# A two-layer hybrid decoder on one core: splitting its float32 weights in the DMA queue of GpSimd instead of on VectorE

## The chip, the core and the metric

The kernel runs on one core of one Trainium2 chip. The metric is the device time of one execution in microseconds (us); less is better. A core has TensorE (PE; the loading of its weights is listed as PEld), VectorE (DVE), ScalarE (ACT), GpSimd (POOL) and SyncE (SP); 16 DMA engines move data between HBM and the core's SBUF.

## The reference

Two post-norm layers over 528 tokens (16 learned ones and 512 real ones) of 2048 channels. A layer is one input projection, three groups of heads that read it side by side, and one output projection:

```python
proj = h @ w_in                                   # 2048 x 5120
c, q, k, v, gates, r_x = split(proj)
y_conv = pointwise(silu(norm(dwconv(glu(c))))) * silu(gate)
y_attn = sliding_window_attention(rope(q), rope(k), v, sinks) * silu(gate)
y_lru  = rg_lru(conv4(r_x)) * silu(gate)
mixed  = concat(y_conv, y_attn, y_lru) @ w_out    # 2048 x 2048
h      = layer_norm(ALPHA * h + mixed)
```

All of it is float32. The last layer gives back the 512 real tokens only.

## The kernel before

**The products.** TensorE takes its operands as float32r, a float32 that is rounded to fewer bits. So every operand is held as two tiles, `hi` (the value rounded) and `lo` (what the rounding left), and a product is three matmuls: hi times hi, hi times lo, lo times hi (`mm3`, L403). The stream (the tokens' channels) is kept with 128 channels on the partitions, so a layer's input is 16 pairs of tiles of 128 x 528.

**The weights.** `weight_list` (L1178) lays all weights in the order of use: 40 column tiles of `w_in`, 4 of the pointwise weight and the output projection, for each layer. A weight is 128 x 2048 float32 in HBM. `weight_load` (L374) loads it in pieces of 128 x 1024 (512 KB) on SyncE's queue into one of two raw buffers (pool `w`). `weight_split` (L382) cuts a piece into halves of 512 columns. For each half it takes two tiles of the pool `u`: ScalarE copies the raw half into the first with rounding, and VectorE subtracts that from the raw half into the second:

```python
yield S(out=wh, in_=r, func=AF.Copy)
yield V("tensor_tensor", out=wl, in0=r, in1=wh.bitcast(F32), op=ALU.subtract)
```

There are 456 halves in all. One half serves 4 of the 16 steps of a product's sum, that is 24 matmuls where the 528 tokens are two ranges of 264 (layer 0, and the first 16 weights of layer 1: 292 halves) and 12 matmuls of 512 columns otherwise. `flow["held"]` counts pairs that are allotted and not yet used up; no more than `flow["ahead"]` are held: 5 as a rule, 14 in the first group of layer 0 (three products side by side, `gemms`, L424), 18 at the end of layer 0 and in the first group of layer 1, 16 in the last chunk of the output.

**The order of the work.** The program is a set of threads (generators). The class `Sched` (L95) merges them into one fixed order for each engine: it takes the step that could start first by an estimate of costs and latencies. Each engine then runs its list in that order and waits by semaphores. An instruction that waits holds back all that stand behind it on its engine; that goes for the DMA issues in SyncE's and GpSimd's lists as well.

**The start.** `x_load` (L475) brings the tokens on SyncE's queue, `x_norm` normalises them, `turn` (L530) transposes them on TensorE and splits them: ScalarE to a tile `t`, VectorE rounds it to `hi`, and the subtraction to `lo` (L547) is GpSimd's for three channel tiles of four. There are four buffers `t`. The first group of products runs in two phases: tokens 0 to 255 (matmuls of 256 columns), then the other 272.

**The end of layer 0.** `output` (L932): 13 products one after another, then the last three side by side in two phases of 264 tokens, with residual and norm behind them on VectorE.

**GpSimd** does nothing else but the subtractions of the start and 8 operations at the very end.

Of the kernel before, what the change touches and what calls it, by code (L numbers as in the profile page):

```python
# [25 lines left out]
NUNITS = 78  # L26
NRAW = 2
# [3 lines left out]
# column tiles of w_in, in the order in which the permutation below lays them out  # L31
# [11 lines left out]
# per-channel parameters: column offsets in the packed array  # L43
# [7 lines left out]
# constants: rope cos, rope sin, band mask of the first block, band mask, identity  # L51
# [3 lines left out]
# query blocks: (first token, queries, pieces of keys, value chunks, mask)  # L55
# [9 lines left out]
# the branches' tiles that are attention's, among recurrence, attention, convolution, attention  # L65
# [29 lines left out]
class Sched:  # L95
    """Threads of instructions (generators), merged into one order per engine by an estimate of when each could start."""
# [16 lines left out]
    # -- tiles --  # L113
# [19 lines left out]
    # -- instructions --  # L133
# [62 lines left out]
    # -- threads --  # L196
# [76 lines left out]
def body(tc, nc, ctx, t):  # L273
# [5 lines left out]
    cp, up, wp, sp_, ap_ = pool("const", 1), pool("units", 1), pool("wraw", 1), pool("small", 1), pool("attn", 1)  # L279
    pp = pool("psum", 1, space=PSUM)  # L280
    k = Sched(tc, nc, {"u": (up, None, NUNITS), "w": (wp, (128, 1024), NRAW), "s": (sp_, (128, 24), 8), "a": (ap_, (128, 4, L), 2), "P": (ap_, (128, L), 8), "t": (ap_, None, 4), "p": (pp, (128, 2, 512), 2), "b": (pp, (128, 512), 4)})
    V, S, G = k.V, k.S, k.G

# [23 lines left out]
    def prepare():  # L307
        """Small parameters worked out once."""
# [4 lines left out]
        for l in range(DEPTH):  # L313
# [3 lines left out]
            # 2 * softplus(-lam) = 2 * (max(-lam, 0) + log1p(exp(-|lam|)))  # L317
# [21 lines left out]
    class Product:  # L339
        """A product in PSUM: pieces of tokens, in banks of one tile or of several."""  # L340
# [10 lines left out]
        def views(self, x):  # L351
            """Pairs of (product, its place in a tile of tokens)."""
            if self.rngs == FULL and len(self.tiles) == 1:
                return [(self.tiles[0][:, :, 0:HALF], x[:, 0:L].rearrange("p (h c) -> p h c", h=2))]
            return [(self.bank(i), x[:, c:c + n]) for i, (_, c, n) in enumerate(self.rngs)]
# [17 lines left out]

    def weight_load():  # L374
        for w, i in pieces:
            m = min(1024, w.src.shape[1] - 1024 * i)
            raw = yield Alloc("w")
            yield k.dma(raw[:, 0:m], w.src[:, 1024 * i:1024 * i + m])
            w.raw.append((raw, m))
            flow["loaded"] += 1  # L380

    def weight_split():  # L382
        for w, i in pieces:
            yield Until(lambda: len(w.raw) > i)
            raw, m = w.raw[i]
            for j in range(0, m, 512):
                yield Until(lambda: flow["held"] < flow["ahead"])
                flow["held"] += 1
                k.wheld = flow["held"]
                wh = yield Alloc("u", F32R, 512, True)  # L390
                wl = yield Alloc("u", F32R, 512, True)
                r = raw[:, j:j + 512]
                yield S(out=wh, in_=r, func=AF.Copy)
                yield V("tensor_tensor", out=wl, in0=r, in1=wh.bitcast(F32), op=ALU.subtract)
                w.parts.append((wh, wl))
            k.release(raw)
# [11 lines left out]
    def gemm(xs, rngs):  # L408
        """sum over k of w[k].T @ xs[k], w the next weight of the stream, xs pairs of parts."""
# [14 lines left out]
    def gemms(count, xs, phases, ready, done, first):  # L424
        """Several products side by side, the tokens in phases; first: all products for each k in turn, read when all is done."""
# [168 lines left out]
    def means(x):  # L594
        """Means over the channels of four tiles from their sum, exact parts against an exact weight."""
# [62 lines left out]
    def keys(y, p, pr):  # L658
        """Both parts of a pair of key heads, twice over the partitions; for the later blocks the meta keys are put before each window."""
# [74 lines left out]
    def scores(y):  # L734
        """Query by key products and their softmax, block by block."""
# [40 lines left out]
    def mix(y):  # L776
        """Probabilities times values; the four query heads of a key head side by side."""
# [43 lines left out]
    def recur(y, j, pr):  # L821
        """Short convolution, gates and the linear recurrence of one tile of channels."""
# [29 lines left out]
        # a = exp(-2 h), sqrt(1 - a * a) = sqrt(tanh(h)) * (1 + a) with h = c * softplus(-lam) * sigmoid / 2  # L852
# [14 lines left out]
    def gate(y, j, pr):  # L867
        """branch * silu(gate), split for the output product."""
# [19 lines left out]
    def project(y, x, ready, phases):  # L888
        """The products of a layer's input projection, in order."""
# [42 lines left out]
    def output(y, x, nx):  # L932
        """Output product with channels on partitions; residual and the norm over channels follow behind."""
# [29 lines left out]
        def gather():  # L963
            """Sums over channels of z less a first mean, and of its square."""
# [199 lines left out]
    with tc.manual_schedule():  # L1164
# [6 lines left out]
        k.run()  # L1171


# passes of the last output product: (chunk of columns, token tiles)
LAST = [(0, [0, 1, 2, 3]), (1, [0, 1, 2, 3]), (2, [0, 1, 2, 3]), (3, [0, 1]), (3, [2]), (3, [3])]


# [110 lines left out]
```

## Time and profile before

| | |
|---|---|
| time of the runs, median (lowest to highest) | 1491.61 us (1491.59 to 1491.63) |
| profiled execution, span | 1493.8 us |
| TensorE busy | 1454.3 us, 97% |
| VectorE busy | 1052.9 us, 70% |
| ScalarE busy | 706.3 us, 47% |
| GpSimd busy | 33.4 us, 2% |
| HBM read | 128.12 MB |

The profile is of one execution. Its span, first to last instruction, is all the profile gives of that execution's time; it is 2.2 us (0.15%) above the median of the runs. Busy time of TensorE is not TensorE at its peak, since matmuls overlap; the number of matmuls in a stretch (the count behind each busy time) tells its pace. In the rows below, `u` are the tiles of the pool `u`, `w` the raw weight buffers, `a` and `P` hold tokens at the start, `t` the tiles of the turn, `p` and `b` are PSUM.

### The profile page before, as it was taken

To read this page: it belongs to the slowest core of one execution; us is meant where nothing else is said; L and a number is where in the kernel's file an instruction comes from. 1 tells how busy PE (TensorE), PEld (TensorE's weight loads), DVE (VectorE), ACT (ScalarE), POOL (GpSimd) and SP (SyncE) were. 2 spreads that over 40 slices of the span, in tenths; PEclk is the share of its full clock that TensorE was granted. 3 is DMA by queue.
4 is the path that set the end of the run, shared out by engine and by line. 5 is a ranking of instruction groups with operands and counts; after the bars stand their busy time and mean duration, and the time that the engine had idled before them with its cause. 6 is when DMAs were issued, how large, how long until landed. Compare 5 with 4: busy or idle time off the path is not lost.

```text
span 1493.8 us, 25183 instructions
## 1 busy us (share of the span) xinstructions
PE 1454.3 (97%) x10028; PEld 1353.5 (91%) x10028; DVE 1052.9 (70%) x2103; ACT 706.3 (47%) x1539; POOL 33.4 (2%) x36
## 2 busy tenths in 40 slices
PE   4999999999999999999999999999999999999996
PEld 3999999999999999999999997998788888888885
DVE  7788999985588444364688889999747864433438
ACT  5422448884377332222368134778735853323211
POOL 2200000000000000000000000000000000000003
PEclk9999999999999999999999999999999999999998
DMA  6312422142222223232433034223332223523323
GB/s 230 94 51 91 135 79 78 58 135 93 85 73 70 85 86 106 75 103 86 127 115 92 24 108 124 78 60 116 92 101 85 71 71 97 157 85 113 108 62 112
DMA packets 56549, 142.32 MB, mean 95 GB/s; under 512 B 12465, under 2 KB 20913, under 8 KB 56433
## 3 DMA queue, kind: packets, MB, share of 16 engines
q1 hardware_dynamic: 56432, 140.73, 30.8%
q8 instruction: 78, 1.28, 0.4%
q14 instruction: 39, 0.31, 0.1%
HBM read 128.12 MB, written 4.19 MB: 89 GB/s over the span
## 4 chain that ended last, share of the span: by engine, by line
PE 86%; DVE 8%; DMA 2%; ACT 2%; issue 1%; SPq 0%; ACTq 0%; DVEq 0%
PE p L184 68%; PE b L184 16%; DVE u L160 5%; DVE a L160 2%; PE b L188 2%; ACT u L174 1%; DMA w<-in_win 1%; DVE s L160 1%; SPq L194 0%; DMA u<-u 0%; DMA a<-in_x 0%; DVE t L160 0%; ACT t L174 0%; DVE P L160 0%; PE p L188 0%
## 5 line engine op out<-in xcount | busy, mean ns | idle before, releaser
L184 PE MATMUL p<-u,u 128*128 128x264 f32 (+3 forms) x7824 | 1183.1, 306 | 5.7 <-DVE u L160 2.9
L184 PEld LDWEIGHTS p<-u,u 128*128 128x128 f32 x7824 | 1066.5, 189 | 63.2 <-DVE u L160 4.6
L160 DVE TENSOR_TENSOR u<-w,u 128x512 fp32r<-128x512 f32 x456 | 306.3, 690 | 171.3 <-ACT u L174 163.3
L174 ACT ACTIVATE u<-w 128x512 fp32r<-128x512 f32 x456 | 273.1, 622 | 237.6 <-DMA w<-in_wout 118.9
L184 PE MATMUL b<-u,u 128*128 128x512 f32 (+6 forms) x1568 | 291.0, 325 | 4.3 <-DVE u L160 2.7
L184 PEld LDWEIGHTS b<-u,u 128*128 128x128 f32 (+2 forms) x1568 | 241.8, 185 | 33.9 <-DVE u L160 4.3
L160 DVE SCALAR_TENSOR_TENSOR a<-u,dp,a 128x527 f32<-128x527 f32 (+14 forms) x240 | 179.8, 750 | 4.2
L174 ACT ACTIVATE P<-P,s 100x257 f32<-100x257 f32 (+5 forms) x240 | 111.2, 479 | 28.7 <-DVE s L160 28.6
L160 DVE TENSOR_TENSOR u<-u,u 128x528 f32<-128x528 f32 (+5 forms) x146 | 100.9, 697 | 20.8 <-ACT u L174 17.9
L174 ACT ACTIVATE u<-p 128x528 f32<-128x528 f32 (+2 forms) x71 | 42.4, 598 | 152.1 <-PE p L184 151.8
L174 ACT ACTIVATE u<-u 64x528 fp32r<-64x528 f32 (+5 forms) x112 | 63.8, 584 | 81.1 <-DVE u L160 75.1
L160 DVE SCALAR_TENSOR_TENSOR u<-u,p 128x528 f32<-128x528 f32 (+3 forms) x45 | 30.8, 684 | 74.3 <-ACT u L174 53.4
L174 ACT ACTIVATE t<-b 128x400 fp32r<-128x400 f32 (+3 forms) x112 | 57.1, 510 | 44.2 <-PE b L184 22.0
L160 DVE CUSTOM_DVE_ANT_0 P<-b,con,nsink 100x256 f32<-100x256 f32 (+2 forms) x160 | 67.3, 451 | 3.0 <-PE b L184 2.2
L160 DVE TENSOR_TENSOR t<-b,t 128x400 fp32r<-128x400 f32 (+2 forms) x72 | 41.7, 580 | 13.5 <-ACT t L174 13.2
L184 PE MATMUL b<-t,u 128*128 128x400 f32 (+2 forms) x144 | 50.5, 351 | 0.0
L167 POOL TENSOR_TENSOR u<-u,P 128x512 f32<-128x512 f32 x8 | 13.1, 1649 | 1412.5 <-ACT u L174 1412.4
L188 PE MATMUL b<-con,P 100*128 100x100 f32 (+2 forms) x320 | 44.1, 253 | 0.0
L174 ACT ACTIVATE u<-b 128x256 fp32r<-128x256 f32 (+4 forms) x28 | 11.8, 443 | 58.5 <-PE b L188 52.0
L188 PEld LDWEIGHTS b<-con,P 100*128 100x128 f32 (+2 forms) x320 | 36.0, 140 | 3.1 <-DVE s L160 0.4
L160 DVE TENSOR_SCALAR P<-P,s 100x256 f32<-100x256 f32 (+3 forms) x88 | 31.6, 364 | 0.7
L160 DVE SCALAR_TENSOR_TENSOR u<-u,u 128x528 f32<-128x528 f32 (+1 forms) x40 | 27.5, 699 | 5.1 <-ACT u L174 4.7
(103 smaller groups left out, 692.1 us busy)
## 6 DMA issues: line engine op xcount, KB each, us to landing
w<-in_win SPq DMA_DIRECT2D x160, 512.0 KB, 3.7
w<-in_wout SPq DMA_DIRECT2D x64, 512.0 KB, 3.8
u<-u SPq DMA_DIRECT2D x48, 120.0 KB, 2.1
a<-in_x SPq DMA_DIRECT2D x8, 256.0 KB, 6.0
P<-in_x SPq DMA_DIRECT2D x8, 256.0 KB, 6.0
u<-u SPq DMA_DIRECT2D x16, 128.0 KB, 2.1
w<-in_pw SPq DMA_DIRECT2D x8, 256.0 KB, 2.6
out<-a SPq DMA_DIRECT2D x8, 256.0 KB, 2.3
```

Of the source, the lines that this page charges most:

```text
L160: return self._op("V", c, outs, ins, lambda: f(**kw))
L167: return self._op("G", c, outs, ins, lambda: f(**kw))
L174: op = self._op("S", c, outs, ins, lambda: f(**kw))
L184: return self._op("T", c, [out], [w, x], lambda: f(out, w, x, start=start, stop=stop))
L188: return self._op("T", max(2 * self._size(ident) / 2400, 0.11) + 0.005, [out], [x, ident], lambda: f(out, x, ident))
```

## The change

The raw buffers and their pool go (the pool `u` gets 81 tiles in place of 78). A half is now loaded by a DMA that GpSimd issues, from HBM straight into the float32r tile `wh`, rounding on the way. ScalarE writes minus that into `wl`. A second DMA of GpSimd reads the same half from HBM once more and adds it onto `wl`. VectorE takes no part. The scheduler's entry for such a DMA is a cost of 1.0 us on GpSimd and 3.0 us of latency. Comments and docstrings are deleted too, which changes nothing.

```diff
-NUNITS = 78
-NRAW = 2
+NUNITS = 81
...
+    def gdma(self, out, in_, add=False):
+
+        f = self.nc.gpsimd.dma_start
+        kw = dict(accum_op=ALU.add) if add else {}
+        ins = [out] if add else []
+        return self._op("G", 1.0, [out], ins, lambda: f(out=out, in_=in_, **kw), 3.0)
...
-    cp, up, wp, sp_, ap_ = pool("const", 1), pool("units", 1), pool("wraw", 1), pool("small", 1), pool("attn", 1)
+    cp, up, sp_, ap_ = pool("const", 1), pool("units", 1), pool("small", 1), pool("attn", 1)
...
+    halves = [(w, j) for w, i in pieces for j in range(1024 * i, min(1024 * i + 1024, w.src.shape[1]), 512)]
+    loading = []
+
     def weight_load():
-        for w, i in pieces:
-            m = min(1024, w.src.shape[1] - 1024 * i)
-            raw = yield Alloc("w")
-            yield k.dma(raw[:, 0:m], w.src[:, 1024 * i:1024 * i + m])
-            w.raw.append((raw, m))
-            flow["loaded"] += 1
+
+        for w, j in halves:
+            yield Until(lambda: flow["held"] < flow["ahead"])
+            flow["held"] += 1
+            k.wheld = flow["held"]
+            wh = yield Alloc("u", F32R, 512, True)
+            wl = yield Alloc("u", F32R, 512, True)
+            yield k.gdma(wh, w.src[:, j:j + 512])
+            loading.append((wh, wl))
+            flow["loaded"] += 0.5
 
     def weight_split():
-        for w, i in pieces:
-            yield Until(lambda: len(w.raw) > i)
-            raw, m = w.raw[i]
-            for j in range(0, m, 512):
-                yield Until(lambda: flow["held"] < flow["ahead"])
-                flow["held"] += 1
-                k.wheld = flow["held"]
-                wh = yield Alloc("u", F32R, 512, True)
-                wl = yield Alloc("u", F32R, 512, True)
-                r = raw[:, j:j + 512]
-                yield S(out=wh, in_=r, func=AF.Copy)
-                yield V("tensor_tensor", out=wl, in0=r, in1=wh.bitcast(F32), op=ALU.subtract)
-                w.parts.append((wh, wl))
-            k.release(raw)
+
+        for n, (w, j) in enumerate(halves):
+            yield Until(lambda: len(loading) > n)
+            wh, wl = loading[n]
+            yield S(out=wl, in_=wh.bitcast(F32), func=AF.Copy, scale=-1.0)
+            yield k.gdma(wl, w.src[:, j:j + 512], add=True)
+            w.parts.append((wh, wl))
```

In the lists below a DMA row names the tile that it writes (pool, buffer and a serial number); of a pair of one half, the load carries the smaller serial number and the adding DMA the next one. `waits` names the semaphores of the engine or DMA lane that the row waits for.

**The start, GpSimd.** Before, its list begins with the subtractions of `turn`, which write the `lo` tiles (`u1`, `u3`, `u5`):

```order
L1284 UNCONDITIONAL_BRANCH [waits barrier_Pool_Activation_PE_DVE_SP_gather]
L167 ISA
L167 TENSOR_TENSOR u1_2_88<-t0_64_204,u0_1_87 128x256 [waits DVE_49]
L167 TENSOR_TENSOR u3_4_90<-t1_65_207,u2_3_89 128x256 [waits DVE_49]
L167 TENSOR_TENSOR u5_6_92<-t2_73_223,u4_5_91 128x256 [waits DVE_49]
```

Now 14 loads and 14 adding DMAs of the first group stand ahead of them; the last of these and the first subtractions are:

```order
L200 DMA u53_68_190<-in_win 128x512 [waits DMASW0_49,Activation_49]
L200 DMA u55_76_205<-in_win 128x512 [waits DMASW1_49,Activation_49]
L200 DMA u57_78_212<-in_win 128x512 [waits DMASW2_49,Activation_49]
L200 DMA u59_80_219<-in_win 128x512 [waits DMASW3_49,Activation_49]
L166 ISA
L166 TENSOR_TENSOR u1_2_85<-t0_89_242,u0_1_84 128x256 [waits DVE_49]
L166 TENSOR_TENSOR u3_4_87<-t1_90_246,u2_3_86 128x256 [waits DVE_49]
L166 TENSOR_TENSOR u5_6_89<-t2_94_262,u4_5_88 128x256 [waits DVE_49]
```

So the `lo` tiles of the tokens moved behind the last adding DMA, which waits for ScalarE. On ScalarE the last passes stand behind the square root of the norm of the last 16 tokens (`s2`):

```order
L173 ACTIVATE s2_93_255<-s2_93_255,cst_74 16x1 [waits DVE_49]
L173 ACTIVATE u55_76_205<-u54_75_204 128x512 [waits DMASW3_49]
L173 ACTIVATE u57_78_212<-u56_77_211 128x512 [waits DMASW4_49]
L173 ACTIVATE u59_80_219<-u58_79_218 128x512 [waits DMASW5_49]
L173 ACTIVATE t0_101_337<-b3_98_299,par_70 128x256 [waits PE_49,Pool_49]
```

What moved: the chain from the last tokens' norm to the first `lo` tile now runs through GpSimd's list.

**In the course of a layer, GpSimd.** Before, its list has nothing here; SyncE's list holds the loads of whole pieces, each waiting for VectorE to be done with the raw buffer:

```order
L194 DMA w0_202_1222<-in_win 128x1024 [waits DMAHW3_49,DVE_49]
L194 DMA w1_207_1285<-in_win 128x1024 [waits DMAHW5_49,DVE_49]
L194 DMA w0_214_1352<-in_win 128x1024 [waits DMAHW6_49,DVE_49]
```

Now loads (they wait for TensorE to free a pair) and adding DMAs (they wait for ScalarE) alternate in one list:

```order
L200 DMA u56_206_1471<-in_win 128x512 [waits DMASW1_49,PE_49]
L200 DMA u58_208_1503<-in_win 128x512 [waits DMASW2_49,PE_49]
L200 DMA u55_203_1438<-in_win 128x512 [waits DMASW3_49,Activation_49]
L200 DMA u57_207_1472<-in_win 128x512 [waits DMASW4_49,Activation_49]
L200 DMA u64_210_1536<-in_win 128x512 [waits DMASW5_49,PE_49]
L200 DMA u59_209_1504<-in_win 128x512 [waits DMASW6_49,Activation_49]
L200 DMA u66_212_1568<-in_win 128x512 [waits DMASW7_49,PE_49]
```

What moved: an adding DMA (`u55`, `u57`) now stands behind one or two later loads, which wait for TensorE.

**The end of layer 0.** Before, VectorE's list holds the subtractions of the weights between those of the residual; the first row here is the residual's of channel tile 12:

```order
L160 TENSOR_TENSOR u20_1219_8840<-u24_25_111,u25_26_112 128x528
L160 TENSOR_TENSOR u33_1218_8839<-w0_1211_8763,u40_1217_8838 128x512 [waits DMAHW1_49,Activation_49]
L160 TENSOR_TENSOR u49_1222_8846<-w0_1211_8763,u21_1221_8845 128x512 [waits Activation_49]
L160 TENSOR_TENSOR u5_1225_8851<-w1_1216_8812,u4_1224_8850 128x512 [waits DMAHW2_49,Activation_49]
L160 TENSOR_TENSOR u15_1227_8856<-w1_1216_8812,u14_1226_8855 128x512 [waits Activation_49]
```

Now 15 loads stand in a row on GpSimd, for the last three products and for the first group of layer 1, and the adding DMAs of all of them behind; the last three loads and the first three adding DMAs are:

```order
L200 DMA u24_1127_8889<-in_win 128x512 [waits DMASW1_49,DVE_49,Pool_49]
L200 DMA u9_1129_8892<-in_win 128x512 [waits DMASW2_49,PE_49]
L200 DMA u57_1131_8895<-in_win 128x512 [waits DMASW3_49,PE_49]
L200 DMA u6_1100_8768<-in_wout0 128x512 [waits DMASW4_49,Activation_49]
L200 DMA u34_1102_8797<-in_wout0 128x512 [waits DMASW5_49,Activation_49]
L200 DMA u13_1104_8825<-in_wout0 128x512 [waits DMASW6_49,Activation_49]
```

What moved: `u6`, needed by the first of the three products, now comes behind the load into `u57`, a buffer that TensorE frees in the product before.

## Rows read from the trace of the kernel before

**Rows 1.** Stretches: each engine's busy us (instructions), granted clock, DMA share, GB/s.

```profile
core 0: us, PE busy (x) PEld busy (x) DVE busy (x) ACT busy (x) POOL busy (x), PEclk, DMA share, GB/s
0.00:25.00 25.00, 7.84 (x28) 4.90 (x28) 17.63 (x42) 13.43 (x24) 4.89 (x10) 1.00 0.80 269
...
225.00:275.00 50.00, 50.00 (x411) 49.56 (x410) 48.97 (x134) 43.32 (x125) 0.00 (x0) 1.00 0.22 67
...
600.00:700.00 100.00, 100.00 (x819) 99.87 (x818) 49.64 (x77) 23.49 (x41) 0.00 (x0) 1.00 0.27 85
...
1225.00:1275.00 50.00, 50.00 (x218) 40.62 (x217) 19.43 (x30) 14.94 (x26) 0.00 (x0) 1.00 0.29 94
```

**Rows 2.** What TensorE waited for, whole span: us in total, times, longest.

```profile
PE b L188 <- ACT a L174: 13.1, 2, 11.3
PE p L184 <- DVE u L160: 3.6, 5, 1.3
PE b L188 <- ACT t L174: 3.0, 4, 2.2
PE b L184 <- DVE u L160: 2.7, 3, 1.6
PE p L184 <- ACT u L174: 2.6, 2, 1.9
```

**Rows 3.** Instructions on the raw buffers: count, ns min/median/max, first and last start.

```profile
L174 ACT ACTIVATE u<-w x456: 612/620/650, 13.6 to 1433.4; 128x512 fp32r<-128x512 f32 x152
L160 DVE TENSOR_TENSOR u<-w,u x456: 628/687/1230, 14.3 to 1434.7; 128x512 fp32r<-128x512 f32 x152
...
DMA to landing us min/median/max: 2.5/3.7/7.1
```

**Rows 4.** The start, in order of time: start us, us, engine, line, instruction.

```profile
0.74 3.71 SPq L194 DMA_DIRECT2D a<-in_x  x8
...
18.72 0.74 POOL L167 TENSOR_TENSOR u<-t,u 128x256 fp32r<-128x256 f32 x1 [18.27 <-DVE u L160]
...
20.29 1.86 POOL L167 TENSOR_TENSOR u<-t,u 128x256 fp32r<-128x256 f32 x2 [0.83 <-DVE u L160]
...
20.34 1.23 DVE L160 TENSOR_TENSOR u<-w,u 128x512 fp32r<-128x512 f32 x1
```

**Rows 5.** Matmuls of L184 alone in two stretches: PE busy (x), PEld busy (x), clock, DMA.

```profile
18.00:34.10 16.10, 8.40 (x27) 6.62 (x28) 1.00 0.44 120
34.10:75.60 41.50, 36.26 (x263) 32.85 (x261) 1.00 0.37 121
```

**Rows 6.** The chain that ended last, around the end of the first group.

```profile
69.68 5.83 DMA w<-in_win
...
75.53 0.63 ACT u L174
...
77.39 22.74 PE p L184 x172
```

**Rows 7.** DMA issues of the whole span: KB each, median us from issue to landing.

```profile
w<-in_wout SPq DMA_DIRECT2D x64, 512.0 KB, 3.8
...
P<-in_x SPq DMA_DIRECT2D x8, 256.0 KB, 6.0
...
w<-in_pw SPq DMA_DIRECT2D x8, 256.0 KB, 2.6
```

**Rows 8.** The DMA queue from 340 to 346 us, one 256 KB load: packets, MB, share.

```profile
q1 hardware_dynamic: 144, 0.26, 16.6%
```

**Rows 9.** The stretch 3 to 17 us, as in Rows 1.

```profile
3.00:17.00 14.00, 1.70 (x6) 0.86 (x6) 9.44 (x20) 6.60 (x12) 0.00 (x0) 1.00 0.97 351
```

**Rows 10.** GpSimd's groups by form: count | busy us, mean ns of one | idle before.

```profile
L167 POOL TENSOR_TENSOR u<-u,P 128x512 f32<-128x512 f32 x8 | 13.1, 1649 | 1412.5 <-ACT u L174 1412.4
...
L167 POOL TENSOR_TENSOR u<-t,u 128x256 fp32r<-128x256 f32 x12 | 10.4, 885 | 23.8 <-DVE u L160 23.8
```

**Rows 11.** VectorE's scaling by a constant for each partition, from the page.

```profile
L160 DVE TENSOR_SCALAR P<-P,s 100x256 f32<-100x256 f32 (+3 forms) x88 | 31.6, 364 | 0.7
```

More of the change, by code (lines that the diff above doesn't have):

```diff
@@ L277, in pool @@
         return ctx.enter_context(tc.tile_pool(name=name, bufs=bufs, **kw))
-    cp, up, wp, sp_, ap_ = pool("const", 1), pool("units", 1), pool("wraw", 1), pool("small", 1), pool("attn", 1)
+    cp, up, sp_, ap_ = pool("const", 1), pool("units", 1), pool("small", 1), pool("attn", 1)
     pp = pool("psum", 1, space=PSUM)
-    k = Sched(tc, nc, {"u": (up, None, NUNITS), "w": (wp, (128, 1024), NRAW), "s": (sp_, (128, 24), 8), "a": (ap_, (128, 4, L), 2), "P": (ap_, (128, L), 8), "t": (ap_, None, 4), "p": (pp, (128, 2, 512), 2), "b": (pp, (128, 512), 4)})
+    k = Sched(tc, nc, {"u": (up, None, NUNITS), "s": (sp_, (128, 24), 8), "a": (ap_, (128, 4, L), 2), "P": (ap_, (128, L), 8), "t": (ap_, None, 4), "p": (pp, (128, 2, 512), 2), "b": (pp, (128, 512), 4)})
     V, S, G = k.V, k.S, k.G
```

## The prediction

> **What bounds the kernel now.** First the table of stretches. TensorE is busy without a gap in all that lies behind the start, at full clock, and its count of matmuls gives the pace: 819 of 264 columns in 100 us, so 0.122 us each, and 218 of 512 columns in 50 us, so 0.229 us [rows 1]. A half of a weight feeds 24 of the first or 12 of the second kind. It is used up in 24 x 0.122 = 2.93 us, or in 12 x 0.229 = 2.75 us; that is the rate at which the new path must deliver. VectorE at 49 of 50 us does not slow TensorE: from 225 to 275 us there are 411 matmuls in 50 us, the full pace [rows 1]. Second, the waits: TensorE waits for VectorE only 3.6 + 2.7 = 6.3 us in the whole run; the longest item, 13.1 us, is the first transposes, which wait for the tokens [rows 2]. So the 306 us of VectorE that go (456 subtractions of 0.687 us [rows 3]) are worth 6.3 us at most: they are hidden already. More than the wait of the start can't be won at all. A measurement of this kernel tells about 2% from no change, 30 us; a gain of that size has no place to come from.
>
> **The path of a half, new.** ScalarE's pass stays (456 of 0.62 us [rows 3]). Gone are the 232 loads of up to 512 KB on SyncE; added are 456 loads and 456 adding DMAs of 256 KB on GpSimd, 912 issues, where its list had nothing. No row shows a DMA of GpSimd, a rounding or an adding one, so I bound each resource.
>
> *Issue on GpSimd.* From below, SyncE's: 8 issues in 3.71 us, 0.46 each [rows 4]. From above, GpSimd's longest work, 1.65 us; its shorter one is 0.885 [rows 10]. I take 0.9, the nearest row on that engine. Two issues make 1.8 us of the 2.75 to 2.93 of a half: hidden. At 1.65 they make 3.3: not hidden. Break-even is 1.4 us.
> The Trainium skill ("DMA: Bandwidth & Descriptors", Latency and other measured facts) gives about 1 us to the first byte from GpSimd's queue and 0.6 from SyncE's; by an estimate of 1 us an issue the sum is the same. No run so far shows it.
>
> *DMA engines.* A load of 256 KB alone had them busy for 16.6% of 6 us, 1.0 us [rows 8]; with the queues full they moved 351 GB/s at a share of 0.97, so 0.72 us for 256 KB [rows 9]. The adding DMA moves no less than a load and reads the tile too, so one to two loads: 0.72 to 2.0 us. I take two loads at the rate of full queues, 1.45, since many are in flight. Load and add then take 2.2 us of 2.75 to 2.93; at the upper ends 3.0, which is over.
>
> *Latency.* Five pairs are held, so a load goes out four uses, 11.0 to 11.7 us, ahead of need. A load lands in 2.6 us (256 KB alone) to 6.0 (256 KB among others); 512 KB take 3.8 [rows 7]. I take 3.3 for the load (2.6 and the slower issue) and 3.8 for the add, which moves as much as 512 KB. In the common order (268 of the 456 halves) one later load stands ahead of the add; it waits for TensorE to free a pair one use later. The add goes out at about 5 us (load 3.3, pass 0.6, waits for ScalarE's other work about 1) and lands at 8.8: in time by over 2 us. In 79 halves two later loads stand ahead; then the add can't go before two uses (5.5 to 5.9 us) and that load's 0.9 us have passed, and has some 4.8 us to land. With 3.8 it does. Landings before reach 7.1 us [rows 3]; if one in ten of the 79 is late by 0.4 us, that is 3 us. I take +3. What is queued behind a held load is always the next add, and TensorE waits for that.
>
> **The start.** GpSimd now makes the tokens' `lo` tiles behind 14 loads and 14 adds. The first stood at 18.7 us [rows 4]. Loads of tokens and constants (4.6 MB) and of 14 halves (3.7 MB) make 8.3 MB; at 351 GB/s [rows 9] they are in by 2.6 + 23.6 = 26 us. Then come the norm of the last tokens (some 3 us on VectorE), ScalarE's pieces up to the last pass (about 3) and the last issue, so the first `lo` tile is made at about 34 us. Before, 27 of the first group's matmuls were done by 34.1 us, and the other 263 took until 75.6 [rows 5]. From 34 us all 290 and 18 transposes more are still to do: 27 x 0.119 + 18 x 0.16 = 6 us later. Against this, TensorE lost 1.9 us from 75.5 to 77.4 to a weight that came late [rows 6]; the new list has that load out long before. Net +4, between 0 and +13 (tokens slowed by the weights' loads, which now run beside them from the first microsecond).
>
> **The middle, the handover, the end.** Of the 6.3 us of waits for VectorE I take 4 as won. At the end of layer 0, the add of the third half of the last three products comes behind a load that TensorE frees 5.9 us before that half is used; load issue 0.9 and landing 3.8 leave a microsecond, and from there halves are used every 1.47 us against 0.9 (issue) or 1.45 (DMA). I take +1; with 2 us an add, 12 halves cost 6. In the last chunk halves are used every 1.4 us, but those 13 adds may go before it begins. The tail of the output does not touch the weights.
>
> **Sum.** +4 (start) - 4 (middle) + 1 (handover) + 3 (late adds) = +4 us on the span of 1493.8; on the median of the runs, 2.2 us lower, 1495.6. So no change.
>
> **The rivals.** *One: the delivery is the bound (slower).* If two issues or two transfers take longer than a half's use, TensorE waits at every half: 456 x (p - 2.85) on top of 1491.6. At p = 3.0, the upper end for the DMA engines, that is +68, 1560 us; at 3.3, the upper end for the issue, +205, 1697. It decides from an issue of 1.4 us or an add of 2.1 us of all engines. For it: GpSimd's own rows of 1.65, and that the adding form is unknown. Against: both middle values leave a fifth of the time free.
> *Two: the rate suffices, but adds land late (slower).* In the order with two loads ahead, each 1 us above 4.8 costs 79 us on top of 1491.6. At 6.0, as loads took at the start [rows 7], +95: 1587; at 5.2, +32: 1524. For it: landings of 6.0 and 7.1 exist. Against: they stand where the queues were full, and the steady share is 0.27 to 0.29 [rows 1], which will rise to about 0.8.
> *Three: a gain.* The start costs nothing, and all waits for VectorE and the late weight go: 1491.6 - 6.3 - 1.9 = 1483. For it: VectorE is relieved at the start as well. Against: the `lo` tiles behind the adds.
> *Four: VectorE holds up GpSimd's issues.* Where the two work side by side, one is slowed: a subtraction that takes 0.69 us took 1.23 beside GpSimd's work at 20.3 us [rows 3, 4]. If each of the 88 scalings of the attention (31.6 us [rows 11]) holds up an add that TensorE needs, the time is 1495.6 + 31.6 = 1527. Against: an issue has about 1 us to spare at each half, a scaling takes 0.36.
> The Trainium skill ("SBUF — State Buffer", SBUF: two separate sides) says that GpSimd can't write the descriptors of its DMAs while VectorE runs an operation on two ports, and advises the queues of SyncE or ScalarE; by this rule rival four would hold. The slowed subtraction agrees that the two engines share something, but shows nothing of a DMA.
>
> **How the numbers follow.** Forecast, 1486 to 1510: 0.56. Rival one 0.17, two 0.18, three 0.07, four 0.02. Rival two splits at its 5.2 us of landing, about 0.08 below 2% and 0.10 above; rivals one and four lie above. Faster by over 2%: 0.01, for what I have not seen. Within 2%: 0.56 + 0.07 + 0.08 less that 0.01, 0.70. Slower: 0.17 + 0.10 + 0.02 = 0.29. The range goes from 1482 (below the gain) to 1590, which takes in nearly all of rival two and the low end of rival one and leaves out some 0.15 above; the likeliest case alone is 1486 to 1510.
>
> **What would show it.** Right: 219 matmuls of 512 columns or 820 of 264 in the same stretches as before; the page lists 912 DMAs of GpSimd, their issue near 0.9 us, loads landing near 3.3 and adds below 4.8; VectorE about 310 us less busy; the first long run of matmuls ends its first group near 81 us. Wrong: TensorE's waits led by DMAs on `u`, spread over all stretches (rival one, with GpSimd or the DMA share near 1), or in a fifth of the halves (rival two), and a first `lo` tile far from 34 us.

## The result, and the profile after

The changed kernel takes 1707.93 us (median; 1707.72 to 1708.14) against 1491.61 us: ratio 1.1446, 95% interval 1.1427 to 1.1464, so 216 us slower. The prediction was 1495.6 us in a range of 1482 to 1590.

The page of the changed kernel: span and busy time, the queue of GpSimd's DMAs, the chain that ended last, GpSimd's issues as instructions (count, busy, mean ns, idle before), and issues with their KB and us to landing.

```profile
span 1705.9 us, 26200 instructions
...
PE 1518.5 (89%) x10028; PEld 1369.3 (80%) x10028; DVE 787.0 (46%) x1647; ACT 719.9 (42%) x1540; POOL 687.0 (40%) x948
...
q0 software_dynamic: 131328, 239.13, 69.6%
...
issue 50%; POOL 34%; PE 5%; DMA 4%; ACT 3%; DVE 2%; POOLq 1%; ACTq 0%
...
L200 POOL DMA_DIRECT2D u<-in_win x640 | 462.3, 861 | 750.6 <-ACT u L173 529.0
...
u<-in_win POOLq DMA_DIRECT2D x640, 256.0 KB, 5.2
u<-in_wout POOLq DMA_DIRECT2D x256, 256.0 KB, 5.1
u<-u SPq DMA_DIRECT2D x48, 120.0 KB, 5.2
```

No engine is full. GpSimd is busy for 40%, and its queue's transfers take 69.6% of the 16 DMA engines; yet the chain that ended last is GpSimd and "issue" for 84% of the span, TensorE for 5%. GpSimd's issues last 0.86 us, as taken, but it stands idle for 750.6 us before DMAs of `in_win` alone, waiting mostly for ScalarE. Every landing is longer than taken. The page's 5.2 us is the median over loads and adds together; told apart by the engine that each issue waits for, the 456 loads land in 5.5 us, where the prediction had 3.3, and the 456 adds in 4.8, where it had 3.8. Even SyncE's small copies inside SBUF, which have nothing to do with the weights, go from 2.1 us on the page before to 5.2.

The stretches of the changed kernel, which answer to [rows 1] and have the same columns (the same time is an earlier place of the program here; only the stretch from 600 to 700 us is compared, where both kernels run matmuls of 264 columns):

```profile
0.00:25.00 25.00, 1.34 (x4) 0.58 (x4) 9.69 (x23) 8.12 (x11) 8.75 (x19) 1.00 1.00 313
25.00:50.00 25.00, 3.66 (x11) 1.76 (x11) 13.75 (x37) 10.02 (x21) 11.20 (x13) 1.00 0.96 178
...
600.00:700.00 100.00, 91.81 (x712) 87.61 (x711) 16.69 (x24) 24.49 (x41) 42.74 (x60) 1.00 0.78 156
1225.00:1275.00 50.00, 45.84 (x194) 34.99 (x193) 7.60 (x16) 16.95 (x31) 23.88 (x33) 1.00 0.85 172
225.00:275.00 50.00, 42.35 (x313) 39.93 (x314) 37.90 (x103) 31.37 (x89) 17.26 (x24) 0.97 0.70 138
```

Two losses show here. In the first 50 us TensorE does 15 matmuls. In the steady stretch it does 712 in 100 us instead of 819: 24 for a half, so 29.7 halves, one in 3.37 us instead of 2.93. Busy time hides that (91.8 of 100), the count shows it. Of the 3.37 us the DMA engines are busy for 0.78, 2.63 us, and idle for 0.74.

Both kernels run 10028 matmuls, so the times by which they have begun as many tell where all of the loss lies. The 541 matmuls that were begun by 100 us in the kernel before are begun by 121 us now; the 5442 by 700 us, by 800; the 6238 by 800 us, by 933; the 9441 by 1350 us, by 1534. Of 212 us between the two spans, the start costs 21, the rest of layer 0 79, the handover to layer 1 33, layer 1 up to 1350 us 51, and the rest 28.

What TensorE and GpSimd waited for in the changed kernel (us in total, times, longest), beside [rows 2]:

```profile
PE b L183 <- DMA u<-in_wout: 27.5, 12, 10.9
PE p L183 <- DMA u<-in_win: 25.4, 38, 3.0
...
PE p L183 <- POOL u L166: 13.0, 1, 13.0
...
POOL u L200 <- ACT u L173: 736.9, 276, 17.4
```

The sum of TensorE's waits for DMAs of weights, some 71 us, is much less than 216: a late weight mostly shows as a slower row of matmuls. What repeats is seen in the timeline of the changed kernel at 1402 us (start, us, engine, instruction, how long it was idle before, and what ended that):

```profile
1402.30 0.63 ACT L173 ACTIVATE u<-u 128x512 fp32r<-128x512 f32 x1 [5.26 <-DMA u<-in_win]
1403.34 0.88 POOL L200 DMA_DIRECT2D u<-in_win  x1 [3.44 <-ACT u L173]
...
1404.31 1.25 ACT L173 ACTIVATE u<-u 128x512 fp32r<-128x512 f32 x2 [1.38 <-DMA u<-in_win]
1405.37 3.51 POOL L200 DMA_DIRECT2D u<-in_win  x5 [1.15 <-ACT u L173]
...
1412.54 0.63 ACT L173 ACTIVATE u<-u 128x512 fp32r<-128x512 f32 x1 [4.39 <-DMA u<-in_win]
1413.58 0.88 POOL L200 DMA_DIRECT2D u<-in_win  x1 [4.71 <-ACT u L173]
```

This is a loop. Three loads land, ScalarE negates, and GpSimd issues six DMAs (adds, and the loads behind them). The next entry of its list is an add, which waits for ScalarE, which waits for a load that only just went out among the adds: it goes out at 1405.92 us and lands at 1412.46, 6.54 us later. Three halves take 1412.54 - 1402.30 = 10.24 us, 3.41 each; TensorE needs 2.75 here.

### The profile page after: what moved, and what is told of

It reads as the page before. It is cut to its first block, busy times and chain, and to the rows that moved or that the text cites. A ratio compares the mean times of both kernels' runs of the same rounds, so it can differ in the third digit from the quotient of the medians.

```text
span 1705.9 us, 26200 instructions
## 1 busy us (share of the span) xinstructions
PE 1518.5 (89%) x10028; PEld 1369.3 (80%) x10028; DVE 787.0 (46%) x1647; ACT 719.9 (42%) x1540; POOL 687.0 (40%) x948
## 3 DMA queue, kind: packets, MB, share of 16 engines
q0 software_dynamic: 131328, 239.13, 69.6%
## 4 chain that ended last, share of the span: by engine, by line
issue 50%; POOL 34%; PE 5%; DMA 4%; ACT 3%; DVE 2%; POOLq 1%; ACTq 0%
POOL u L200 34%; DMA u<-in_win 3%; PE p L183 2%; PE b L183 1%; DMA u<-in_wout 1%; DVE a L159 1%; ACT u L173 1%; ACT P L173 1%; PE b L187 1%; DVE u L159 1%; ACT t L173 1%; POOLq L200 1%; DVE spq L159 0%; DVE P L159 0%; ACT L173 0%
## 5 line engine op out<-in xcount | busy, mean ns | idle before, releaser
L183 PE MATMUL p<-u,u 128*128 128x264 f32 (+3 forms) x7824 | 1211.0, 308 | 60.3 <-DMA u<-in_win 25.4
L200 POOL DMA_DIRECT2D u<-in_win x640 | 462.3, 861 | 750.6 <-ACT u L173 529.0
L173 ACT ACTIVATE u<-u 128x512 fp32r<-128x512 f32 (+4 forms) x568 | 344.8, 620 | 761.6 <-DMA u<-in_win 439.7
L183 PE MATMUL b<-u,u 128*128 128x264 f32 (+6 forms) x1568 | 307.3, 334 | 47.0 <-DMA u<-in_wout 27.5
L200 POOL DMA_DIRECT2D u<-in_wout x256 | 184.6, 851 | 216.1 <-ACT u L173 191.2
L183 PE MATMUL b<-t,u 128*128 128x400 f32 (+2 forms) x144 | 55.1, 383 | 18.9 <-ACT t L173 18.0
L183 PEld LDWEIGHTS b<-t,u 128*128 128x128 f32 x144 | 27.8, 193 | 29.9 <-ACT t L173 25.6
L159 DVE TENSOR_TENSOR u<-u,b 128x512 f32<-128x512 f32 x6 | 4.1, 682 | 79.1 <-issue 79.1
L187 PE MATMUL b<-con,a 128*128 128x128 f32 x32 | 8.8, 371 | 33.2 <-DMA con<-in_con 17.9
## 6 DMA issues: line engine op xcount, KB each, us to landing
P<-in_x SPq DMA_DIRECT2D x8, 256.0 KB, 11.2
```

What stands on the lines that cost most here:

```text
L159: return self._op("V", c, outs, ins, lambda: f(**kw))
L173: op = self._op("S", c, outs, ins, lambda: f(**kw))
L183: return self._op("T", c, [out], [w, x], lambda: f(out, w, x, start=start, stop=stop))
L187: return self._op("T", max(2 * self._size(ident) / 2400, 0.11) + 0.005, [out], [x, ident], lambda: f(out, x, ident))
L200: return self._op("G", 1.0, [out], ins, lambda: f(out=out, in_=in_, **kw), 3.0)
```

## The experiments

Twelve kernels, each in three rounds against the kernel before, whose median there was 1492.0 us. They test four theories: A, a chain of waits through GpSimd's list (A1) or through the five pairs (A2); B, the bytes; C, the adding; and the start by itself. e2, e7 and e11 leave the adding out, so their output is not the product asked for.

| run | us | ratio to before (95%) |
|---|---|---|
| e1: loads early in the list, 7 pairs | 1554.0 | 1.040 to 1.043 |
| e2: no add | 1518.9 | 1.017 to 1.020 |
| e3: two loads side by side | 1517.5 | 1.016 to 1.019 |
| e4: SyncE loads, GpSimd adds | 1577.3 | 1.054 to 1.061 |
| e5: list order only | 1626.5 | 1.088 to 1.092 |
| e6: 7 pairs only | 1694.0 | 1.131 to 1.140 |
| e7: plain load in the add's place | 1536.1 | 1.029 to 1.032 |
| e8: 4 pairs | 1712.2 | 1.142 to 1.150 |
| e9: start only | 1670.5 | 1.118 to 1.122 |
| e10: start and early loads | 1534.8 | 1.027 to 1.030 |
| e11: the wait without the add | 1516.2 | 1.014 to 1.017 |
| e12: as e10, 8 pairs | 1537.7 | 1.028 to 1.032 |

### First four: list, bytes or adding

e1, loads early:

```diff
-AHEAD = 5
+AHEAD = 7
-        return self._op("G", 1.0, [out], ins, lambda: f(out=out, in_=in_, **kw), 3.0)
+        return self._op("G", 1.0, [out], ins, lambda: f(out=out, in_=in_, **kw), 5.5)
```

> The changed kernel with the planner told that a DMA of GpSimd's queue takes 5.5 us to land instead of 3.0, so that it writes more loads ahead of each add in GpSimd's list, and with 7 pairs of tiles held instead of 5. Same bytes, same work. Theory A (latency: a pair lives through two landings of 5.2 us each and an add waits at the head of GpSimd's list until the load before it has landed, so the loads behind it go out late): with 7 pairs a half may live 7 x 2.85 = 20 us, more than 5.2 + 0.6 + 0.9 + 5.2 + 2.9 = 14.8 us, so the time falls by most of the loss, to 1510 to 1590 us. Theory B (the 16 DMA engines can't move two fetches of each half faster than one half in 3.2 us): nothing more to be had, 1680 to 1720 us. Theory C (the adding DMA alone is slow) goes with B here.

e2, no add:

```diff
             yield S(out=wl, in_=wh.bitcast(F32), func=AF.Copy, scale=-1.0)
-            yield k.gdma(wl, w.src[:, j:j + 512], add=True)
             w.parts.append((wh, wl))
```

> The changed kernel without the adding DMA: the lower half is left at minus the rounded weight, so the output is not the product asked for, but the loads, ScalarE's pass and TensorE's work stay. Half the bytes, half of GpSimd's issues, one landing instead of two in a row, and nothing in GpSimd's list that waits for ScalarE. All theories expect most of the loss to go: A and B 1490 to 1520 us. If it stays above 1600 us the loads by GpSimd's queue alone are the cause.

e3, two loads side by side (`weight_raw` is the loop of the kernel before that loads `raw` by SyncE):

```diff
-            yield S(out=wl, in_=wh.bitcast(F32), func=AF.Copy, scale=-1.0)
-            yield k.gdma(wl, w.src[:, j:j + 512], add=True)
+            yield V("tensor_tensor", out=wl, in0=raw[:, o:o + 512], in1=wh.bitcast(F32), op=ALU.subtract)
```

> Each half is still fetched twice, but side by side: GpSimd's queue loads the rounded half, SyncE's queue loads it raw into two raw buffers as in the kernel before (78 units), and VectorE subtracts. No adding DMA, no ScalarE pass. The bytes from HBM are those of the changed kernel (239 MB), the chain of two landings in a row is gone, and GpSimd's list holds loads alone. Theory A (latency chain): 1490 to 1540 us. Theory B (two fetches are too much for the DMA engines): 1650 to 1710 us. Theory C (the adding DMA is what is slow): 1490 to 1540 us, like A.

e4, SyncE loads (`weight_load` and the raw buffers as before):

```diff
                 yield S(out=wh, in_=r, func=AF.Copy)
-                yield V("tensor_tensor", out=wl, in0=r, in1=wh.bitcast(F32), op=ALU.subtract)
+                yield S(out=wl, in_=wh.bitcast(F32), func=AF.Copy, scale=-1.0)
+                yield k.gdma(wl, w.src[:, 1024 * i + j:1024 * i + j + 512], add=True)
```

> The raw halves come by SyncE's queue into two raw buffers as in the kernel before (78 units), ScalarE rounds them and writes the negative, and the adding DMA of GpSimd's queue stays, alone in its list. Bytes, adds and the landing of an add are those of the changed kernel; only the landing of the load lies outside the life of a pair, and no load stands behind an add. Theory A (latency chain through GpSimd's list): a pair lives 0.6 + 0.6 + 0.9 + 5.2 + 2.9 = 10.2 us, under 5 x 2.85 = 14.3, so 1500 to 1560 us. Theory B (bytes): 1650 to 1710 us. Theory C (the adding DMA is slow in itself): 1620 to 1710 us. A against C is told by this run and the one with two loads side by side together.

Measured: 1554.0, 1518.9, 1517.5 and 1577.3 us. With the same bytes, e1 takes back 154 of the 216 us by the order of the list and the pairs, so B falls. e3 says so again: 239 MB of weights, in two queues, cost 1.7%. e4 came between the ranges of A and C; from 600 to 700 us it ran at the full 820 matmuls, so its loss lies elsewhere (385 matmuls in the first 100 us against 541 before, 156 x 0.122 = 19 us). By the count of equal matmuls 19 us more are lost between 150 and 275 us of the kernel before, and 44 between 700 and 1000; why is not shown. e2 and e4 give the prices of the two kinds of DMA, in the lines of GpSimd's queue on their pages (packets, MB, share of the 16 engines' span). First e2, loads alone:

```profile
q0 software_dynamic: 65664, 119.57, 30.6%
```

Then e4, adds alone:

```profile
q0 software_dynamic: 65664, 119.57, 46.9%
```

A plain load: 0.306 x 1515.8 / 456 = 1.02 us of all 16 engines. An add of as many bytes: 0.469 x 1575.9 / 456 = 1.62 us. Together they make 2.64; the changed kernel's own line gives 0.696 x 1705.9 / 456 = 2.60 for the two.

### List order, pairs, adding

For each add, count the loads that stand ahead of it in GpSimd's list beyond its own (the adds with none or with more than three are left out here):

| kernel | one | two | three |
|---|---|---|---|
| changed kernel | 268 | 79 | 9 |
| e5 | 188 | 186 | 10 |
| e6 | 270 | 79 | 9 |
| e8 | 330 | 14 | 9 |
| e1 | 78 | 258 | 55 |

e5 is e1 with 5 pairs, e6 is the changed kernel with `AHEAD = 7`, e8 with `AHEAD = 4`. e7 has loads and second DMAs in the very order of the changed kernel:

```diff
-            yield k.gdma(wl, w.src[:, j:j + 512], add=True)
+            yield k.gdma(wl, w.src[:, j:j + 512])
```

> The changed kernel with one number altered: the planner takes 5.5 us instead of 3.0 for the landing of a DMA of GpSimd's queue. 5 pairs as before. In GpSimd's list, the adds that stand behind just one later load fall from 268 to 188, those behind two rise from 79 to 186. Theory A1 (the list: an add at its head waits for its own load to land and for ScalarE, and the loads behind it wait with it; with one later load out the loop is about 7.8 us for two halves, 3.9 each, with two out 2.6 each, which is under TensorE's need): 80 to 107 halves gain about 1.0 us, so 1600 to 1630 us. Theory A2 (the pairs: a pair lives 14.8 to 15.8 us and there are 5, 3.0 to 3.2 us per half, whatever the list says): 1660 to 1710 us.

> The changed kernel with 7 pairs held instead of 5 and the planner's landing left at 3.0 us. The order of GpSimd's list hardly moves: 270 adds behind one later load (268 in the changed kernel), 79 behind two (79). Theory A1 (the order of the list): 1680 to 1715 us, no change. Theory A2 (the number of pairs): 15.8 / 7 = 2.3 us per half, so 1510 to 1580 us.

> The changed kernel with the second DMA of each half as a plain load over the negative, without the addition, so that the lower half holds the rounded weight and the output is not the product asked for. Order of the lists, waits, bytes and number of DMAs are those of the changed kernel. It prices the adding itself: plain loads took 1.02 us of all 16 engines each in the run without adds (30.6% of 1515.8 us over 456), adds 1.62 us in the run with SyncE's loads (46.9% of 1575.9 us over 456). Theory A1 (the list): the loop of a load's landing stays, but the landing may shorten to the 4.2 us of the run with two loads side by side, so about 0.5 us less on some 270 halves: 1570 to 1660 us. Theory C (the adding is the whole loss): 1515 to 1535 us. Theory B (bytes): 1690 to 1710 us.

> The changed kernel with 4 pairs held instead of 5. In GpSimd's list 330 adds stand behind one later load (268 in the changed kernel) and 14 behind two (79). Theory A1 (the list): 62 to 65 halves lose about 1.0 to 1.3 us each, 1770 to 1790 us. Theory A2 (the pairs): 15.8 / 4 = 3.95 us per half instead of 3.2, about 340 us more, 1900 to 2050 us. Theory B (engines): no change, 1690 to 1720 us.

Measured: 1626.5, 1694.0, 1536.1 and 1712.2 us. e5 fell inside A1's range and e6 too (two more pairs that leave the list as it is give 14 us; A2 wanted over 120). So the list counts, and more pairs by themselves do little. Under the early list two more pairs are worth 73 us (e5 to e1), but they change the list as well (258 adds behind two loads, against 186), and the two are not told apart there. And e8 contradicts A1's arithmetic: 62 more adds behind a single load cost 4 us and not the 62 or more that it gives. Landings are shorter there (loads 5.05 us instead of 5.53, adds 4.41 instead of 4.80), which pays a part of it back; the rest is open. And e7, with the list's order unchanged, took back 172 us, more than A1 allowed and nearly what C allowed. Neither theory alone is right. The stretch 600 to 700 us puts them side by side. Columns as in [rows 1]; first e7, the plain load in the add's place:

```profile
600.00:700.00 100.00, 100.00 (x820) 99.87 (x819) 27.70 (x41) 27.44 (x45) 35.45 (x67) 1.00 0.68 181
```

e5, the order alone:

```profile
600.00:700.00 100.00, 98.97 (x800) 97.81 (x799) 25.19 (x37) 27.96 (x47) 48.68 (x68) 1.00 0.86 174
```

e8, four pairs:

```profile
600.00:700.00 100.00, 93.70 (x736) 90.41 (x736) 16.61 (x24) 25.07 (x41) 43.05 (x60) 1.00 0.80 159
```

The engines' time for a half (share x 100 us / halves) is 0.78 x 3.37 = 2.63 us in the changed kernel, 2.6 in e5 and e8, and 2.0 in e7 (0.68 x 2.93). TensorE uses a half in 2.93. So 0.3 us of each half may be lost in idle engines; the loop above loses 0.74. Shorten the adds by 0.6, or lose less in the loop, and TensorE is at its pace again.

In e7 the same loop turns faster. ScalarE's negations there, as in the timeline above:

```profile
1405.30 0.63 ACT L173 ACTIVATE u<-u 128x512 fp32r<-128x512 f32 x1 [3.73 <-DMA u<-in_wout]
1407.24 1.28 ACT L173 ACTIVATE u<-u 128x512 fp32r<-128x512 f32 x2 [1.31 <-DMA u<-in_wout]
1412.23 0.63 ACT L173 ACTIVATE u<-u 128x512 fp32r<-128x512 f32 x1 [3.70 <-DMA u<-in_wout]
```

Three halves in 6.93 us instead of 10.24. These rows are of `w_out`; among the loads of `w_in`, as in the changed kernel's rows, a turn takes 6.96 us (from 1264.38). The load that ends it goes out at 1267.69 us and lands at 1271.26, 3.57 us instead of 6.54, which is 3.0 of the 3.3 us between the turns. Over the whole run loads land in 4.0 us in e7 and in 5.5 in the changed kernel: a load lands later when adds are moved beside it.

### The wait alone, the start, and what is left

e9 and e10 take the first 14 halves as in the kernel before; e10 and e12 have the numbers of e1 beside (e12: 8 pairs, 7.0 us):

```diff
-            yield k.gdma(wh, w.src[:, j:j + 512])
+            if len(loading) < 14:
+                raw = yield Alloc("u", F32, 512, True)
+                yield k.dma(raw, w.src[:, j:j + 512])
+            else:
+                yield k.gdma(wh, w.src[:, j:j + 512])
...
+            if raw is not None:
+                yield S(out=wh, in_=raw, func=AF.Copy)
+                yield V("tensor_tensor", out=wl, in0=raw, in1=wh.bitcast(F32), op=ALU.subtract)
+                k.release(raw)
```

e11, the wait without the add:

```diff
-            yield k.gdma(wl, w.src[:, j:j + 512], add=True)
+            yield G("tensor_tensor", out=wl[:, 0:8], in0=wl[:, 0:8].bitcast(F32), in1=wh[:, 0:8].bitcast(F32), op=ALU.add)
```

> The changed kernel with its first 14 halves taken as in the kernel before: loaded raw by SyncE's queue into single tiles (at most 4 at a time), rounded by ScalarE, subtracted by VectorE. From half 15 on all is as in the changed kernel (267 adds behind one later load, 77 behind two). In the first 100 us the changed kernel had done 369 matmuls against 543 of the kernel before, 174 x 0.122 = 21 us. If the start is a loss of its own: 1680 to 1695 us. If the later stretches, where weights come too late anyway, take it all back: 1700 to 1715 us.

> The start of the run before this one (first 14 halves by SyncE, ScalarE and VectorE) together with loads written earlier into GpSimd's list (planner's landing 5.5 us, 7 pairs). 442 of the 456 halves still come by load and adding DMA. If start and list are the two causes and add up: 1554 - 21, so 1525 to 1545 us. If the adds have a price beyond both (engines busy 0.83 to 0.95 in the run with early loads), the time stays near 1545 to 1560 us.

> The changed kernel with each adding DMA replaced by a GpSimd instruction on 8 columns of the same two tiles, which waits for ScalarE as the add did: GpSimd's list keeps its wait, the second fetch goes. (The lower half is then minus the rounded weight but for those columns, so the output is not the product asked for.) If the wait in the list is the loss by itself: 1600 to 1690 us. If it costs only together with the adds, which make each landing longer: a plain load lands in 3.3 us (the run without adds), so the loop with one later load out is 3.3 + 0.25 + 0.63 + 0.4 + 0.6 = 5.2 us for two halves, 2.6 each, under TensorE's 2.75 to 2.93, and the time is that of the run without adds, 1510 to 1530 us.

> As the run with start and early loads, with 8 pairs and a planner's landing of 7.0 us: adds behind two later loads 166, behind three 190 (250 and 56 with 7 pairs and 5.5 us). If what is left there is still the list: 1500 to 1525 us. If it is the 16 engines (load 1.02 + add 1.62 us = 2.64 us per half against TensorE's 2.75 to 2.93, with SyncE's own transfers beside): no change from that run, 1525 to 1550 us.

Measured: 1670.5, 1534.8, 1516.2 and 1537.7 us. e11 shows GpSimd waiting more than ever, and TensorE at its pace. Its waits and its stretch (0.34 x 2.93 = 1.0 us of engines for a half):

```profile
POOL u L166 <- ACT u L173: 890.4, 315, 31.7
...
600.00:700.00 100.00, 100.00 (x818) 99.87 (x818) 27.03 (x40) 26.16 (x43) 25.95 (x68) 1.00 0.34 93
```

Its list is no looser than the changed kernel's: 110 of the 456 waits stand behind no later load and 285 behind one, against 55 and 268. So a wait of 890 us in GpSimd's list costs nothing beyond e2's 1.8% where a load lands in 3.3 us. In the steady stretch the wait and the adds do harm only together, since e4, with the adds and no loads behind them, was at its pace there too.

e9 gave back 37 us, more than the 21 expected and below both ranges; with its 577 matmuls in the first 100 us against 369, 25 us of it are seen there. The other 12 come up to 700 us, where e9 loses 67 us from 100 us on and the changed kernel 79; why is not shown. Three things made the start late. They show in the time of the first `lo` tile, 18.7 us before [rows 4]. In e3 GpSimd's list has the 14 loads and no second DMAs:

```profile
28.50 1.63 POOL L167 TENSOR_TENSOR u<-t,u 128x256 fp32r<-128x256 f32 x2 [10.94 <-DVE s L160]
```

In e7 14 plain DMAs stand behind the loads, each waiting for ScalarE:

```profile
42.11 2.78 POOL L166 TENSOR_TENSOR u<-t,u 128x256 fp32r<-128x256 f32 x4
```

In the changed kernel these are adds, and TensorE waits 13 us for the tile after its first weight matmul:

```profile
37.63 0.56 PE L183 MATMUL p<-u,u 128*128 128x256 f32 x1
...
50.10 3.09 POOL L166 TENSOR_TENSOR u<-t,u 128x256 fp32r<-128x256 f32 x4
51.20 1.43 PE L183 MATMUL p<-u,u 128*128 128x256 f32 x5 [13.01 <-POOL u L166]
```

So 10 us by loads that run beside the tokens' own (the later tokens land in 11.2 us instead of 6.0 [rows 7]; in e9 in 5.5), 14 us more by 14 second DMAs that wait in turn ahead of the `lo` tiles, and 8 us by their adding. (e11, with three waits ahead of that tile, has it at 29.1 us; e2 at 36.8, but its ScalarE makes the first `t` 7 us later than the changed kernel's.)

e10 keeps 442 of 456 halves on the new path and is 43 us over the kernel before; e12 has no less, as the theory of the engines expected, so more pairs and an earlier list don't help further. In e10 the steady stretch is at pace with the engines busier:

```profile
600.00:700.00 100.00, 100.00 (x820) 99.87 (x819) 28.66 (x42) 26.28 (x43) 48.94 (x69) 1.00 0.88 181
...
725.00:750.00 25.00, 18.87 (x147) 18.65 (x146) 8.06 (x14) 10.74 (x20) 13.74 (x22) 0.89 1.00 229
750.00:775.00 25.00, 24.89 (x192) 24.23 (x192) 4.51 (x10) 3.30 (x6) 11.10 (x14) 0.98 0.83 141
775.00:800.00 25.00, 11.84 (x65) 9.41 (x64) 24.06 (x63) 21.49 (x45) 12.76 (x19) 0.71 0.92 190
```

Most of what is left stands at the handover: 605 matmuls from 700 to 800 us against 798 in the kernel before, 193 x 0.122 = 24 us (TensorE is busy for 80.6 us of these 100, at a mean granted clock of 0.89). There the list has loads, then adds in a row. GpSimd's timeline of e10:

```profile
738.09 3.56 POOL L200 DMA_DIRECT2D u<-in_win  x6
742.75 0.88 POOL L200 DMA_DIRECT2D u<-in_wout  x1 [1.11 <-ACT a L173]
744.68 0.90 POOL L200 DMA_DIRECT2D u<-in_wout  x1 [1.04 <-ACT u L173]
746.08 0.87 POOL L200 DMA_DIRECT2D u<-in_wout  x1 [0.49 <-ACT u L173]
747.89 0.85 POOL L200 DMA_DIRECT2D u<-in_wout  x1 [0.94 <-ACT u L173]
749.92 0.86 POOL L200 DMA_DIRECT2D u<-in_wout  x1 [1.19 <-ACT u L173]
751.62 0.86 POOL L200 DMA_DIRECT2D u<-in_wout  x1 [0.84 <-issue]
753.06 0.86 POOL L200 DMA_DIRECT2D u<-in_wout  x1 [0.57 <-issue]
755.67 0.85 POOL L200 DMA_DIRECT2D u<-in_wout  x1 [1.75 <-issue]
```

Adds one after the other go out 1.85 us apart ((755.67 - 742.75) / 7), while halves are wanted every 1.47 us, so the adds can't keep up there. How much of the 1.85 is the engines (at 0.83 to 1.00) and how much ScalarE, which the adds wait for, is not separated, and a list without that cluster was not tried. Another 47 matmuls of 512 columns are missing from 1400 to 1500 us (403 against 450 in the 100 us before them; 47 x 0.229 = 11 us), where the last chunk has such a cluster too; that this is the same cause is argued, not shown.

The count of equal matmuls gives the loss of each kernel by stretches of the kernel before, in us (the last one up to the end of the span):

| kernel | 0 to 100 | to 700 | to 800 | to 1350 | to the end |
|---|---|---|---|---|---|
| changed kernel | 21 | 79 | 33 | 51 | 28 |
| e5: list order | 21 | 22 | 32 | 38 | 19 |
| e1: list order, 7 pairs | 20 | -1 | 24 | 2 | 11 |
| e10: e1 and the start | -3 | 5 | 24 | 3 | 11 |
| e7: plain DMA for the add | 13 | 10 | 13 | 2 | 7 |
| e11: waits without adds | 4 | 9 | 2 | 5 | 0 |

List and pairs take back the long stretches and little of the handover and the end; those two go with the adds (e11), and plain DMAs in their place still cost 13 and 7 us (e7). No version here beats the kernel before.

## Why the prediction was wrong, point by point

- **No gain to be had: right.** VectorE lost 1052.9 - 787.0 = 266 us of busy time, and no run here is faster for it. (The prediction's 306 us is a slip: 456 x 0.687 is 313; nothing hangs on it.)
- **Issue on GpSimd, 0.9 us: right.** 0.861 and 0.851 on the mean, with the next issue beginning before the last one ends (five take 3.51 us in the timeline above), and GpSimd is busy for 40%.
- **DMA engines, 2.2 us for load and add: mechanism right, a fifth too small.** 1.02 + 1.62 = 2.64. It stays under 2.93, as was said; but the slack is 0.3 us and not 0.7, and there the conclusion "a fifth of the time free" went wrong.
- **Latency, +3 us: the step that failed.** "The add goes out at about 5 us ... and lands at 8.8: in time by over 2 us" takes each half by itself, with 3.3 and 3.8 us to land. Measured: 5.5 and 4.8, and 6.5 for the load that ends the turn shown above. The 3.3 was right without adds (e2's median), and wrong beside them. The Trainium skill ("DMA: Bandwidth & Descriptors", Anatomy of one DMA — SWDGE (gpsimd) path) fits a DMA of this queue by 2.0 us and its bytes over 436 GB/s, which is 2.6 us for 256 KB by my estimate. The runs have 3.3 without adds and 5.5 for a load here, and the measurement decides. The larger fault: "what is queued behind a held load is always the next add" looked at adds behind a held load, and not at loads behind a held add. An add that waits for its own load keeps back the next loads, so the landing is paid once in each turn of the loop instead of being hidden by the pairs held. The steady part of the loss, 79 us in layer 0 and 51 in layer 1 where the prediction had +3, is that loop on engines with little slack: with the list and the pairs changed (e1) the two stretches cost -1 and 2 us, with the adding alone gone (e7) 10 and 2.
- **The start, +4 (0 to +13): too small by 17.** TensorE is 21 us behind at 100 us. The first `lo` tile, taken at 34 us, is made at 50.1: the price of the loads beside the tokens is in the 34, but the 14 adds' waits in turn for ScalarE and for landings were left out, though they stood ahead of the tiles in the list.
- **The handover, +1 (6 at most): too small.** 33 us in the changed kernel and 24 even in e10, where adds in a row go out 1.85 us apart, not 0.9 or 1.45.
- **The last chunk, put at nothing: wrong.** Behind 1350 us of the kernel before another 28 us are lost; that the 13 adds "may go before it begins" was not worked out. Without the adds (e11) nothing is lost there, with plain DMAs in their place (e7) 7 us.
- **The rivals.** One had the size: 3.3 us for a half gives 1697 on the arithmetic given, but that is luck: it has neither start nor handover in it, and it asked for a full GpSimd or full engines, and neither was. Two had the landing, 5.2, and gave 1524 for it, since it charged 79 halves and not a loop over all. Each held a part; their combination was missing, so the range ended 118 us too low. Three is out. Four was tested by no run of its own and wasn't needed: with GpSimd's loads and waits kept and only the adds gone (e11), the loss is 1.5%.

## What to carry to other kernels

Where one queue holds loads and work that depends on those loads, read its list as a loop: the time of a turn is a landing plus the dependent steps, shared by the loads that go out in one turn. Here the order in the list changed it, and more buffers without a new order gave 14 us of 216. Compare that with the engines' slack, not with their busy share: 0.78 busy was enough to lose 13% of the pace. And take a landing from a stretch as loaded as the new one will be; an adding DMA took 1.6 times the engines' time of a plain one of the same bytes here, and what landed beside it landed later: SyncE's copies in 5.2 us, against 4.3 beside as many plain DMAs (e7) and 2.8 beside the loads alone (e2).

## What was not expected of the hardware

- An adding DMA of 256 KB takes 1.62 us of all 16 engines, a plain rounding load 1.02 (e4, e2).
- GpSimd issues a plain load in 0.527 us (median, e7), an add in 0.865 (e4). Where both are in the list the median over the two is 0.87, but there an issue begins before the one ahead of it ends, so this is not their pace: five took 3.51 us.
- TensorE's granted clock was below its upper level of 2.4 GHz in stretches with wide gaps and not in those with narrow ones: its mean is 0.71 in e10 from 775 to 800 us, where TensorE was busy for 11.8 of 25 us, and 1.00 in the changed kernel from 600 to 700 us, where it was busy for 91.8 of 100. Over the span it was 0.978 in the changed kernel against 0.996 before.
